# Output projection of a hybrid encoder layer: from 384-column blocks of single token tiles to 512-column blocks of pairs, three pairs by Strassen's seven products

## The chip, the cores and the metric

One core of one Trainium2 chip. The metric is device time in microseconds of one execution. The kernel before took 657.14 us, the median of three runs (655.28 to 658.43).

## What is computed

One encoder layer is applied to two sequences, a sample of 1024 tokens and a prompt of 512 tokens, each 1024 wide, in float32:

```python
h = rms_norm(x, norm_g)
proj = h @ w_in
u_pool, g_pool, q, k, v, g_attn = jnp.split(proj, ...)
pool_out = pool_mixer(u_pool, w_pool, pool_scale) * jax.nn.silu(g_pool)
attn_out = neighbourhood_attention(q, k, v, rpb) * jax.nn.silu(g_attn)
mixed = jnp.concatenate([pool_out, attn_out], axis=-1)
return x + mixed @ w_out
```

The change concerns the last line: `mixed` (1536 tokens in all, 1024 wide) times `w_out` (1024 x 1024), plus the residual `x`.

## The kernel before

**Precision.** Every float32 operand of a large matmul is split into a high part in the matmul's fast format (fp32r) and a low part that holds the rest (`split`, L426: the high part by ScalarE or VectorE, the low part by VectorE or GpSimd). A product is three matmuls into the same PSUM accumulator (`mm3`, L454): high by high, high by low, low by high.

**Stages.** The sample is done first and then the prompt, each in four passes over pairs of heads (L781 and L817). A pass loads a block of `w_in` and projects q, k and v (`project_qkv`), then the gates (`gate`, L631) and the pool input (`u_block`, L707), and does the attention of two heads (`attention`, L641) and one group of the pooling mixer (`pooling`, L715). Results go to a DRAM tensor `mixed` per sequence, channels on partitions. The output projection comes last (L828 to L861).

**The output projection.** `w_out` is cut into column blocks of 384, 384 and 256. For each block its eight chunks of 128 rows are loaded and split (`load_w`, L443). Then all 12 tiles of 128 tokens (8 of the sample, 4 of the prompt) go by: one accumulator each, eight chunks, three matmuls a chunk. The tokens' rows of `mixed` are loaded and split once, in the first block, into 24 half tiles `mt`, and all of them stay. The result leaves by a VectorE add of `x` from PSUM (tile `xr`) and a DMA of the block.

**What sets the order.** Nothing is issued while the program text runs. `Plan` records each operation, and `Plan.order` (L228) simulates the five engines with estimated durations (`Plan.cost`, L118) and issues in the order that the simulation gives, so every instruction has line L329 in the profile. When an engine is free it takes, of the operations whose inputs are ready, the one with the lowest priority number, then the one that comes first in the text. FIRST is -1 (weight splits, adds that free a PSUM accumulator), 0 is the default (attention and pooling among it), MAIN is 1: the large projections, which are also kept in the order of the text among themselves. So the large matmuls fill whatever TensorE time attention leaves. Within `plan.choice()` an operation goes to that engine on which it would end sooner. On the chip every engine runs its list in order.

**Buffers.** Tiles come from rings (`ring`, `big`, `halves`, `staged`): a new tile of a ring waits until all uses of the tile that many places before are done. The rings that matter here: `ht` with 16 slots of 2 x 512, holding the transposed inputs and later `mt`; `big` with 6 slots of 4 KB a partition; `w` with 10 and `wr` with 5 slots for weights and their raw loads; `raw` with 2 slots; `tree` with 2, used by the pooling; `qkv` with 4. PSUM has eight banks: three for `acc`, two each for `s` and `pt` and one for `po`, the last three used by attention.

Of the kernel before, what the change touches and what calls it, by code (L numbers as in the profile page):

```python
# [332 lines left out]
FIRST = -1  # L333
MAIN = 1
# [3 lines left out]
def encoder(ctx, tc, xn_p, xt_p, xn_s, xt_s, w_in, w_out, w_pool, pscale, ng, qg, kg,  # L338
            rpb, rpbm, negs, ident_d, ones_d, edge_d, y_p, y_s):
    plan = Plan(tc.nc)  # L340
# [18 lines left out]
    def staged(name):  # L359
        return ring("raw", 2, [P, 512], name)  # L360
# [65 lines left out]
    def split(out_h, out_l, src, scale=None):  # L426
        with plan.choice():
            act.activation(out=out_h, in_=src, func=AF.Copy, scale=1.0 if scale is None else scale)
            if scale is None:
                dve.tensor_copy(out=out_h, in_=src)  # L430
        low(out_l, src, out_h, scale)

    def low(out, src, high, scale=None):
        if scale is not None:
            dve.scalar_tensor_tensor(out=out, in0=src, scalar=scale, in1=high.bitcast(F32),
                                     op0=ALU.mult, op1=ALU.subtract)
            return
        with plan.choice():
            dve.tensor_tensor(out=out, in0=src, in1=high.bitcast(F32), op=ALU.subtract)
            if src.space != PSUM:  # L440
                pool.tensor_tensor(out=out, in0=src, in1=high.bitcast(F32), op=ALU.subtract)

    def load_w(blk, width, nm, chunks=range(KC), queue=sp):  # L443
        ws = []
        for k in chunks:
            raw = ring("wr", RAWS, [P, BW], f"wr_{nm}_{k}")[:, 0:width]
# [7 lines left out]
    def mm3(out, ah, al, bh, bl, first, last):  # L454
        pe.matmul(out, lhsT=ah, rhs=bh, start=first, stop=False)
        pe.matmul(out, lhsT=ah, rhs=bl, start=False, stop=False)
        pe.matmul(out, lhsT=al, rhs=bh, start=False, stop=last)
# [26 lines left out]
    ns_edge = {cb: sb.tile([P, 384], F32, name=f"ns_edge_{cb}") for cb in (0, 3)}  # L484
# [4 lines left out]
    class Sequence:  # L489
# [160 lines left out]
        def head_rows(self, p, hd, rt, bt):  # L650
# [4 lines left out]
            for cb in range(4):  # L655
# [13 lines left out]
                pe.matmul(sv, lhsT=q[:, hd, qo:qo + P], rhs=kv(k[:, hd]), start=True, stop=False)  # L669
                pe.matmul(sv, lhsT=q[:, hd, qo:qo + P], rhs=kv(k[:, 2 + hd]), start=False, stop=True)  # L670
# [158 lines left out]
    mts = {}  # L829
    f0 = 0  # L830
    for bi, fw in enumerate((384, 384, 256)):
        w = load_w(w_out[:, :, f0:f0 + fw], fw, f"o{bi}")
        for i, (sq, t, xn, y) in enumerate(toks):
            if bi == 0:
                mts[i] = []
                for hf in range(2):
                    nm = f"mt_{i}_{hf}"
                    if i < 8:
                        m = halves(nm)
                    elif i < 11:  # L840
                        m = big([P, 2, 512], nm, F32R)
                    else:
                        m = ring("v", 4, [P, 2, 512], nm, F32R)
                    if i < 5:
                        raw = staged(f"mr_{i}_{hf}")
                    else:
                        raw = bias[i % 2][:, hf * 512:hf * 512 + 512]
                    sp.dma_start(out=raw.rearrange("p (k s) -> p k s", s=P),
                                 in_=sq.mixed.rearrange("k p s -> p k s")[:, 4 * hf:4 * hf + 4, t * P:(t + 1) * P])
                    split(m[:, 0], m[:, 1], raw)  # L850
                    mts[i].append(m)
            acc = bank("acc", f"acco_{bi}_{i}")
            with plan.priority(MAIN):
                for c in range(KC):
                    m, mc = mts[i][c // 4], slice((c % 4) * P, (c % 4 + 1) * P)
                    mm3(acc[:, 0:fw], m[:, 0, mc], m[:, 1, mc], w[c][:, 0], w[c][:, 1], c == 0, c == KC - 1)
            xr = ring("qkv", QBUFS, [P, BW], f"xr_{bi}_{i}")[:, 0:fw]
            sp.dma_start(out=xr, in_=xn[t * P:(t + 1) * P, f0:f0 + fw])
            dve.tensor_tensor(out=xr, in0=acc[:, 0:fw], in1=xr, op=ALU.add)
            sp.dma_start(out=y[t * P:(t + 1) * P, f0:f0 + fw], in_=xr)  # L860
        f0 += fw  # L861
# [64 lines left out]
```

## Time and profile before

| | |
|---|---|
| median of three runs | 657.14 us (655.28 to 658.43) |
| the profiled execution | 655.92 us |
| its span, first to last instruction | 654.1 us |
| TensorE busy (PE) | 644.7 us, 99% |
| VectorE busy (DVE) | 514.6 us, 79% |
| ScalarE busy (ACT) | 346.4 us, 53% |
| GpSimd busy (POOL) | 64.3 us, 10% |
| moved by DMA | 97.35 MB, 149 GB/s |
| first matmul of the output projection | 510.0 us |

PE is TensorE's matmuls, PEld its weight loads, SP the engine that issues the DMAs. Names such as `acco<-w_o,mt` are the tiles that an instruction writes and reads: `acc_s` and `acc_p` are the q, k, v projections of sample and prompt, `accg` the gates, `accu` the pool inputs, `acco` the output projection, `s`, `pt` and `po` attention. Matmuls overlap in TensorE, so the mean duration of one is longer than the time that it takes from the next.

### The profile page before, as it was taken

What the parts mean: (1) busy time and instruction counts of PE and PEld (TensorE: products, weight loads), DVE (VectorE), ACT (ScalarE), POOL (GpSimd) and SP (SyncE); (2) the same over time, 40 slices, a digit from 0 to 9 for tenths busy, and PEclk for the clock granted to TensorE, in tenths of its full rate; (3) what the DMA queues carried; (4) which work ended last, traced back from release to release, by engine and by line L of the source; (5) the groups of instructions that cost most, each with busy time, mean ns of one, the idle gap of its engine ahead of it and who ended that gap; (6) DMA issues with size and microseconds to landing.
All of it is one profiled execution on the core that took longest, in us unless ns stands there. A gap on an engine that the chain in (4) does not pass through costs nothing.

```text
span 654.1 us, 11733 instructions
## 1 busy us (share of the span) xinstructions
PE 644.7 (99%) x3728; PEld 600.6 (92%) x3728; DVE 514.6 (79%) x1569; ACT 346.4 (53%) x837; POOL 64.3 (10%) x105
## 2 busy tenths in 40 slices
PE   6999999999999999999999999999999999999997
PEld 6998899989899888999889889899898999999997
DVE  6689899899987899969999889899999985411211
ACT  5755777567664666445686457674766740100100
POOL 1130101000000000100012310111211100000000
PEclk9999999999999999999999999999999999999999
DMA  8974254342374422425344544546556666533222
GB/s 291 351 216 138 93 182 120 117 122 83 95 234 139 149 75 61 139 94 171 93 118 145 154 149 149 160 151 193 167 176 208 195 206 217 157 98 98 85 93 73
DMA packets 90657, 97.35 MB, mean 149 GB/s; under 512 B 12644, under 2 KB 82404, under 8 KB 90596
## 3 DMA queue, kind: packets, MB, share of 16 engines
q1 hardware_dynamic: 90596, 96.61, 47.9%
q8 instruction: 29, 0.48, 0.3%
q14 instruction: 32, 0.26, 0.1%
HBM read 77.21 MB, written 19.37 MB: 148 GB/s over the span
## 4 chain that ended last, share of the span: by engine, by line
PE 98%; DMA 1%; DVE 0%; ACT 0%; issue 0%; SPq 0%; ACTq 0%
PE acc_s L329 21%; PE acco L329 21%; PE accg_s L329 14%; PE acc_p L329 10%; PE accu_s L329 7%; PE accg_p L329 7%; PE po_s L329 4%; PE accu_p L329 3%; PE pt_s L329 3%; PE s_s L329 3%; PE po_p L329 1%; PE s_p L329 1%; PE pt_p L329 1%; PE ptq_s L329 1%; PE accm_s L329 1%; PE ptq_p L329 1%
## 5 line engine op out<-in xcount | busy, mean ns | idle before, releaser
L329 PE MATMUL acc_s<-w_sA,ht_s 128*128 128x384 f32 x768 | 146.1, 343 | 5.9 <-DVE w_sA L329 5.9
L329 PEld LDWEIGHTS acc_s<-w_sA,ht_s 128*128 128x128 f32 x768 | 135.9, 191 | 7.2 <-ACT ht_s L329 5.5
L329 PE MATMUL acco<-w_o,mt 128*128 128x384 f32 (+1 forms) x864 | 136.8, 318 | 0.0
L329 PEld LDWEIGHTS acco<-w_o,mt 128*128 128x128 f32 x864 | 133.9, 188 | 0.5 <-DVE w_o L329 0.3
L329 PE MATMUL accg_s<-ht_s,w_sT 128*128 128x512 f32 x384 | 100.7, 399 | 0.0
L329 PEld LDWEIGHTS accg_s<-ht_s,w_sT 128*128 128x128 f32 x384 | 70.0, 188 | 11.9
L329 DVE TENSOR_TENSOR xr<-acco,xr 128x384 f32<-128x384 f32 (+1 forms) x36 | 18.3, 511 | 78.9 <-PE acco L329 78.9
L329 PE MATMUL acc_p<-w_pA,ht_p 128*128 128x384 f32 x384 | 77.6, 341 | 0.0
L329 PEld LDWEIGHTS acc_p<-w_pA,ht_p 128*128 128x128 f32 x384 | 65.9, 188 | 0.8
L329 PE MATMUL accu_s<-ht_s,w_sT 128*128 128x512 f32 x192 | 52.0, 398 | 0.0
L329 PE MATMUL accg_p<-ht_p,w_pT 128*128 128x512 f32 x192 | 46.2, 392 | 0.0
L329 ACT ACTIVATE w_o<-wr_o 128x384 fp32r<-128x384 f32 (+1 forms) x20 | 9.5, 485 | 67.7 <-PE acco L329 61.9
L329 PEld LDWEIGHTS accg_p<-ht_p,w_pT 128*128 128x128 f32 x192 | 35.7, 188 | 7.3
L329 ACT ACTIVATE k<-ptq_s,gqk 64x256 fp32r<-64x256 f32 x64 | 30.0, 470 | 22.1 <-PE ptq_s L329 21.3
L329 PEld LDWEIGHTS accu_s<-ht_s,w_sT 128*128 128x128 f32 x192 | 34.8, 188 | 5.4
L329 ACT ACTIVATE ns_s<-ns_s,sm_s 128x384 f32<-128x384 f32 x52 | 31.2, 610 | 7.5 <-DVE sm_s L329 7.1
L329 DVE TENSOR_TENSOR pp_s<-pt_s,pp_s 128x384 fp32r<-128x384 f32 x64 | 34.5, 545 | 0.5 <-ACT pp_s L329 0.4
L329 ACT ACTIVATE ns_edge<-ns_edge,sm_s 128x288 f32<-128x288 f32 x50 | 26.3, 530 | 15.8 <-DVE sm_s L329 15.4
L329 PE MATMUL po_s<-pp_s,v 128*128 128x256 f32 x192 | 32.2, 287 | 0.1
L329 PEld LDWEIGHTS po_s<-pp_s,v 128*128 128x128 f32 x192 | 28.9, 188 | 2.2 <-ACT w_pT L329 0.4
L329 PE MATMUL s_s<-k,q 128*128 128x288 f32 (+1 forms) x128 | 30.5, 327 | 0.0
L329 ACT ACTIVATE qkv_s<-acc_s,rr_s 128x384 f32<-128x384 f32 x24 | 13.8, 580 | 26.3 <-PE acc_s L329 22.6
(194 smaller groups left out, 1111.3 us busy)
## 6 DMA issues: line engine op xcount, KB each, us to landing
v<-vd_s SPq DMA_DIRECT2D x64, 128.0 KB
wr_sA<-in_w_in SPq DMA_DIRECT2D x32, 192.0 KB
wr_sT<-in_w_in SPq DMA_DIRECT2D x32, 192.0 KB
wr_pA<-in_w_in SPq DMA_DIRECT2D x32, 192.0 KB
wr_pT<-in_w_in SPq DMA_DIRECT2D x32, 192.0 KB
out<-xr SPq DMA_DIRECT2D x24, 192.0 KB
x<-in_xt_s SPq DMA_DIRECT2D x16, 256.0 KB
vd_s<-vt_s SPq DMA_DIRECT2D x32, 128.0 KB
```

The lines of the kernel that those rows point to most:

```text
L329: op.fn()
```

## The change

The 12 token tiles are taken in six pairs, and the columns in two halves of 512. `w_out` is then 2 x 2 blocks of 512 x 512 (B11, B12, B21, B22), and a pair's rows of `mixed` are 2 x 2 blocks of 128 x 512 (token by channel half).

The first three pairs (`PLAIN = 3`) are done plainly: for a pair and a column half two accumulators, four products of four chunks. The last three pairs use the Winograd form of Strassen's algorithm: seven products in place of eight, each again three matmuls a chunk. With S1 = A21 + A22, S2 = S1 - A11, S3 = A11 - A21, S4 = A12 - S2 and T1 = B12 - B11, T2 = B22 - T1, T3 = B22 - B12, and T4 = B21 - T2:

- C11 = A11 B11 + A12 B21
- C12 = A11 B11 + S2 T2 + S1 T1 + S4 B22
- C21 = A11 B11 + S2 T2 + S3 T3 + A22 T4
- C22 = A11 B11 + S2 T2 + S3 T3 + S1 T1

Sums of products are formed where they can be by accumulating on in a PSUM bank whose intermediate value has been read out: A11 B11 is copied to SBUF by ScalarE (`p1`) and added to the three residual tiles by GpSimd; VectorE adds bank b2 to a residual tile after S2 T2 and again after S3 T3. The first Strassen pair (`late`) does S4 B22 early and has it copied and subtracted (`p3`). The T's are made once from a second load of `w_out`, the S's for each pair, and all of them are split into high and low parts like the rest.

With this go changes of buffers: q and k become six tiles of a ring `kq`, which the T's take over; in the order of the `big` ring `sg` and `ph` change places, so that `sg` takes the slot of the second `more` tile (copies of the first pass's q, k, v) in place of `ph`; residual tiles and copies (`piece`) come from the rings `tree`, `pp` and `raw`; B and part of T lie in `ht`, which no longer holds all rows. Two estimates of `Plan.cost` change: GpSimd's power function, which this kernel doesn't use, and GpSimd's other operations, now 200 ns plus the elements' time in place of 135.

```diff
-                return 1600
-            return 135 + n * (2.35 if out.dtype == F32R else 1.85)
+                return 715 + n * 119
+            return 200 + n * (2.35 if out.dtype == F32R else 1.85)
...
-    sg = big([P, 1024], "sg")
+    ph = big([P, 2, 512], "ph", F32R)
     U = big([P, 2 * 528], "U")
     sgp = big([P, 1024], "sgp")
-    ph = big([P, 2, 512], "ph", F32R)
+    sg = big([P, 1024], "sg")
...
-    q = sb.tile([P, 2, 1024], F32R, name="q")
-    k = sb.tile([P, 4, 1024], F32R, name="k")
+    q = [ring("kq", 6, [P, 1024], f"q_{i}", F32R) for i in range(2)]
+    k = [ring("kq", 6, [P, 1024], f"k_{i}", F32R) for i in range(4)]
...
+    def raw_part(nm, i, j, c, half):
+        nm = f"{nm}_{c}_{half}"
+        raw = (ring("qkv", QBUFS, [P, BW], nm) if half and nm[1] == "T" else raw_w(nm))[:, 0:256]
+        o = 512 * j + 256 * half
+        sp.dma_start(out=raw, in_=w_out[:, 4 * i + c, o:o + 256])
+        return raw
+    def weights(nm, i, j, new):
+        with plan.priority(FIRST):
+            ws = [new(f"{nm}_{c}") for c in range(4)]
+            for c, w in enumerate(ws):
+                for half in range(2):
+                    cols = slice(256 * half, 256 * half + 256)
+                    split(w[:, 0, cols], w[:, 1, cols], raw_part(f"r{nm}", i, j, c, half))
+        return ws
...
+    def tt(out, a, b, op):
+        with plan.choice():
+            for eng in (dve, pool):
+                eng.tensor_tensor(out=out, in0=a, in1=b, op=op)
...
+    def product(acc, a, w, first, last, **kw):
+        with plan.priority(MAIN):
+            for c in range(4):
+                mm3(acc, a.chunk(0, c), a.chunk(1, c), w[c][:, 0], w[c][:, 1], first and c == 0, last and c == 3, **kw)
...
+    def leave(tok, j, acc, x):
+        _, t, _, y = toks[tok]
+        with plan.priority(FIRST):
+            dve.tensor_tensor(out=x, in0=acc, in1=x, op=ALU.add)
+        sp.dma_start(out=y[t * P:(t + 1) * P, j * 512:(j + 1) * 512], in_=x)
...
+    B = {(0, 1): weights("B12", 0, 1, halves)}
+    plain, left = {}, [halves(f"left_{i}") for i in range(4)]
...
+    def plain_block(tok, j):
+        accs = [bank("acc", f"acco_{tok + r}_{j}") for r in range(2)]
+        for hf in range(2):
+            for r in range(2):
+                product(accs[r], plain[tok + r][hf], B[hf, j], hf == 0, hf == 1)
+        for r in range(2):
+            leave(tok + r, j, accs[r], x_piece(tok + r, j))
+    for tok in range(4):
+        plain_rows(tok, left if tok < 2 else None)
+        if tok == 1:
+            B[1, 1] = weights("B22", 1, 1, halves)
+            B[0, 0] = weights("B11", 0, 0, halves)
+            B[1, 0] = weights("B21", 1, 0, lambda nm: big([P, 2, 512], nm, F32R))
+    for tok, j in ((0, 1), (2, 1), (0, 0), (2, 0)):
+        plain_block(tok, j)
+    if PLAIN == 3:
+        for tok in (4, 5):
+            plain_rows(tok, left)
+        for j in range(2):
+            plain_block(4, j)
+    T1, T2, T3, T4 = T = [[], [], [], []]
+    for c in range(4):
+        t1, t2, t3, t4 = [(ring("kq", 6, [P, 2, 512], f"T_{c}_{i}", F32R) if 4 * c + i < 6 else
+                           ring("v", 4, [P, 2, 512], f"T_{c}_{i}", F32R) if 4 * c + i < 10 else
+                           big([P, 2, 512], f"T_{c}_{i}", F32R) if 4 * c + i < 12 else
+                           halves(f"T_{c}_{i}")) for i in range(4)]
+        for half in range(2):
...
+            tt(b22, b22, b12, ALU.subtract)
+            tt(b12, b12, b11, ALU.subtract)
+            tt(b11, b22, b11, ALU.add)
+            tt(b21, b21, b11, ALU.subtract)
...
+    for tok in range(2 * PLAIN, 12, 2):
+        odd, late = tok // 2 % 2, tok == 2 * PLAIN
...
+        a11, s1, s2, a12, s3 = [Rows(f"{n}_{tok}") for n in ("A11", "S1", "S2", "A12", "S3")]
+        a22, s4 = [Rows("", t) for t in left[2 * odd:2 * odd + 2]]
...
+        b1, b2, b3 = [bank(("s", "s", "pt")[i] if odd else "acc", f"acco_{tok}_{i}") for i in range(3)]
...
+        product(b1, a11, B[0, 0], True, False, **part)
+        with plan.priority(FIRST):
+            act.activation(out=p1, in_=b1, func=AF.Copy)
+        pool.tensor_tensor(out=x21, in0=x21, in1=p1, op=ALU.add)
+        if late:
+            product(b3, s4, B[1, 1], True, False, **part)
...
+        product(b2, s2, T2, True, False, **part)
+        with plan.priority(FIRST):
+            dve.tensor_tensor(out=x12, in0=b2, in1=x12, op=ALU.add)
+        pool.tensor_tensor(out=x12, in0=x12, in1=p1, op=ALU.add)
+        product(b1, a12, B[1, 0], False, True, **part)
+        leave(tok, 0, b1, x11)
+        product(b2, s3, T3, False, False, **part)
+        with plan.priority(FIRST):
+            dve.tensor_tensor(out=x22, in0=b2, in1=x22, op=ALU.add)
+        pool.tensor_tensor(out=x22, in0=x22, in1=p1, op=ALU.add)
...
+        product(b3, s1, T1, not late, late, **part)
+        leave(tok + 1, 1, b3, x22)
...
+        product(b2, a22, T4, False, True, **part)
+        leave(tok + 1, 0, b2, x21)
+        if not late:
+            product(b3, s4, B[1, 1], False, True, **part)
+            leave(tok, 1, b3, x12)
```

More of the change, by code (lines that the diff above doesn't have):

```diff
@@ L40 @@
 QBUFS = 4
+PLAIN = 3
 class Plan:
@@ L441, in low, with raw_w @@
                 pool.tensor_tensor(out=out, in0=src, in1=high.bitcast(F32), op=ALU.subtract)
+    def raw_w(name):
+        return ring("wr", RAWS, [P, BW], name)
     def load_w(blk, width, nm, chunks=range(KC), queue=sp):
@@ L445, in load_w @@
         for k in chunks:
-            raw = ring("wr", RAWS, [P, BW], f"wr_{nm}_{k}")[:, 0:width]
+            raw = raw_w(f"wr_{nm}_{k}")[:, 0:width]
             queue.dma_start(out=raw, in_=blk[:, k])
@@ L452, in load_w, with mm3 @@
         return ws
[L454 to L457, printed above, removed]
+    def mm3(out, ah, al, bh, bl, first, last, **kw):
+        pe.matmul(out, lhsT=ah, rhs=bh, start=first, stop=False, **kw)
+        pe.matmul(out, lhsT=ah, rhs=bl, start=False, stop=False, **kw)
+        pe.matmul(out, lhsT=al, rhs=bh, start=False, stop=last, **kw)
     def rsqrt(y, t, ms):
@@ L614, in project_qkv @@
                     for rows in (own[hd], own[1 - hd]):
-                        v = q[rows, hd, qa].rearrange("p (cb r c) -> p r cb c", cb=4, r=8)
+                        v = q[hd][rows, qa].rearrange("p (cb r c) -> p r cb c", cb=4, r=8)
                         q_dst.append(v[:, lo::-1, :, ::-1] if hi < 0 else v[:, lo:hi:-1, :, ::-1])
@@ L618, in project_qkv @@
                     for rows in (own[hd], own[1 - hd]):
-                        act.activation(out=k[rows, hd, ka], in_=k_src[hd], func=AF.Copy, scale=gqk[own[hd]])
+                        act.activation(out=k[hd][rows, ka], in_=k_src[hd], func=AF.Copy, scale=gqk[own[hd]])
                     act.activation(out=q_dst[2 * hd], in_=q_src[hd], func=AF.Copy)
                 for hd in range(2):
-                    low(k[own[hd], 2 + hd, ka], k_src[hd], k[own[hd], hd, ka], gqk[own[hd]])
+                    low(k[2 + hd][own[hd], ka], k_src[hd], k[hd][own[hd], ka], gqk[own[hd]])
                     low(q_dst[2 * hd + 1], q_src[hd], q_dst[2 * hd])
@@ L668, in head_rows @@
                 sv = s[:, 0:self.kt_rows * n]
-                pe.matmul(sv, lhsT=q[:, hd, qo:qo + P], rhs=kv(k[:, hd]), start=True, stop=False)
-                pe.matmul(sv, lhsT=q[:, hd, qo:qo + P], rhs=kv(k[:, 2 + hd]), start=False, stop=True)
+                pe.matmul(sv, lhsT=q[hd][:, qo:qo + P], rhs=kv(k[hd]), start=True, stop=False)
+                pe.matmul(sv, lhsT=q[hd][:, qo:qo + P], rhs=kv(k[2 + hd]), start=False, stop=True)
                 ns = (ns_edge[cb] if cb in ns_edge else ring("ns", 2, [P, 384], f"ns_{nm}"))[:, 0:KEYS]
@@ L774, in encoder @@
     for hd in range(2):
-        pool.memset(k[HD - hd * HD:P - hd * HD, 2 + hd].bitcast(F32), 0.0)
+        pool.memset(k[2 + hd][HD - hd * HD:P - hd * HD].bitcast(F32), 0.0)
     for t in ns_edge.values():
@@ L825, in encoder @@
         pr.pooling(p)
-    toks = [(ss, t, xn_s, y_s) for t in range(8)] + [(pr, t, xn_p, y_p) for t in range(4)]
[L829 to L861, printed above, removed]
@@ new lines, in encoder, with __init__, parts, span @@
+    class Rows:
+        def __init__(self, nm, tile=None):
+            self.tiles = [tile] if tile else [ring("w", WBUFS, [P, 2, 256], f"{nm}_{i}", F32R) for i in range(2)]
+            self.n = 4 // len(self.tiles)
+        def parts(self, raw):
+            for i, x in enumerate(self.tiles):
+                n = P * self.n
+                split(x[:, 0, 0:n], x[:, 1, 0:n], raw[:, i * n:i * n + n])
+            return self
+        def span(self, part, c, n=2):
+            return self.tiles[c // self.n][:, part, c % self.n * P:(c % self.n + n) * P]
+        def chunk(self, part, c):
+            return self.span(part, c, 1)
@@ new lines, in tt, with row_raw @@
+    def tt(out, a, b, op):
+        with plan.choice():
+            for eng in (dve, pool):
+                eng.tensor_tensor(out=out, in0=a, in1=b, op=op)
+    def row_raw(raw, tok, half):
+        sq, t = toks[tok][:2]
+        sp.dma_start(out=raw.rearrange("p (k s) -> p k s", s=P),
+                     in_=sq.mixed.rearrange("k p s -> p k s")[:, 4 * half:4 * half + 4, t * P:(t + 1) * P])
+        return raw
+    def product(acc, a, w, first, last, **kw):
+        with plan.priority(MAIN):
+            for c in range(4):
+                mm3(acc, a.chunk(0, c), a.chunk(1, c), w[c][:, 0], w[c][:, 1], first and c == 0, last and c == 3, **kw)
@@ new lines, in encoder, with piece, x_piece @@
+    spare = [0]
+    def piece(nm):
+        i = spare[0]
+        spare[0] += 1
+        tag = "t" if i < 4 * PLAIN else "prt"[i // 2 % 3]
+        return (ring("pp", 2, [P, 512], nm) if tag == "p" else
+                ring("tree", 2, [P, 528], nm)[:, 0:512] if tag == "t" else staged(nm))
+    def x_piece(tok, j):
+        _, t, xn, _ = toks[tok]
+        x = piece(f"xr_{tok}_{j}")
+        sp.dma_start(out=x, in_=xn[t * P:(t + 1) * P, j * 512:(j + 1) * 512])
+        return x
+    def leave(tok, j, acc, x):
[3 more added lines that the diff above has]
+        sp.dma_start(out=y[t * P:(t + 1) * P, j * 512:(j + 1) * 512], in_=x)
@@ new lines, in encoder, with plain_rows @@
+    toks = [(ss, t, xn_s, y_s) for t in range(8)] + [(pr, t, xn_p, y_p) for t in range(4)]
+    B = {(0, 1): weights("B12", 0, 1, halves)}
+    plain, left = {}, [halves(f"left_{i}") for i in range(4)]
+    def plain_rows(tok, tiles=None):
+        plain[tok] = [Rows(f"a_{tok}_{hf}", tiles and tiles[2 * (tok % 2) + hf]).parts(
+            row_raw(staged(f"ra_{tok}_{hf}"), tok, hf)) for hf in range(2)]
+    def plain_block(tok, j):
[5 more added lines that the diff above has]
+            leave(tok + r, j, accs[r], x_piece(tok + r, j))
@@ new lines, in encoder @@
+    T1, T2, T3, T4 = T = [[], [], [], []]
[5 more added lines that the diff above has]
+        for half in range(2):
+            cols = slice(256 * half, 256 * half + 256)
+            b11, b12, b22, b21 = [raw_part(f"rT{i}{j}", i, j, c, half) for i, j in ((0, 0), (0, 1), (1, 1), (1, 0))]
+            tt(b22, b22, b12, ALU.subtract)
+            tt(b12, b12, b11, ALU.subtract)
+            tt(b11, b22, b11, ALU.add)
+            tt(b21, b21, b11, ALU.subtract)
+            for x, raw in zip((t1, t2, t3, t4), (b12, b11, b22, b21)):
+                split(x[:, 0, cols], x[:, 1, cols], raw)
+        for x, t in zip((t1, t2, t3, t4), T):
+            t.append(x)
@@ new lines, in encoder @@
+    for tok in range(2 * PLAIN, 12, 2):
+        odd, late = tok // 2 % 2, tok == 2 * PLAIN
+        (r11, r12), (r21, r22) = [[row_raw(bias[r][:, hf * 512:hf * 512 + 512], tok + r, hf) for hf in range(2)]
+                                  for r in range(2)]
+        a11, s1, s2, a12, s3 = [Rows(f"{n}_{tok}") for n in ("A11", "S1", "S2", "A12", "S3")]
+        a22, s4 = [Rows("", t) for t in left[2 * odd:2 * odd + 2]]
+        a11.parts(r11)
+        a22.parts(r22)
+        a12.parts(r12)
+        tt(r22, r21, r22, ALU.add)
+        tt(r21, r11, r21, ALU.subtract)
+        tt(r11, r22, r11, ALU.subtract)
+        tt(r12, r12, r11, ALU.subtract)
+        if late:
+            s4.parts(r12)
+        s2.parts(r11)
+        s3.parts(r21)
+        s1.parts(r22)
+        if not late:
+            s4.parts(r12)
+        part = dict(skip_group_check=True)
+        b1, b2, b3 = [bank(("s", "s", "pt")[i] if odd else "acc", f"acco_{tok}_{i}") for i in range(3)]
+        p1 = piece(f"p1_{tok}")
+        x11, x12, x21, x22 = [x_piece(tok + r, j) for r in range(2) for j in range(2)]
+        product(b1, a11, B[0, 0], True, False, **part)
+        with plan.priority(FIRST):
+            act.activation(out=p1, in_=b1, func=AF.Copy)
+        pool.tensor_tensor(out=x21, in0=x21, in1=p1, op=ALU.add)
+        if late:
+            product(b3, s4, B[1, 1], True, False, **part)
+            p3 = piece(f"p3_{tok}")
+            with plan.priority(FIRST):
+                act.activation(out=p3, in_=b3, func=AF.Copy)
+        product(b2, s2, T2, True, False, **part)
[5 more added lines that the diff above has]
+        product(b2, s3, T3, False, False, **part)
+        with plan.priority(FIRST):
+            dve.tensor_tensor(out=x22, in0=b2, in1=x22, op=ALU.add)
+        pool.tensor_tensor(out=x22, in0=x22, in1=p1, op=ALU.add)
+        if late:
+            pool.tensor_tensor(out=x22, in0=x22, in1=p3, op=ALU.subtract)
+        product(b3, s1, T1, not late, late, **part)
+        leave(tok + 1, 1, b3, x22)
+        if late:
+            leave(tok, 1, b3, x12)
+        product(b2, a22, T4, False, True, **part)
+        leave(tok + 1, 0, b2, x21)
+        if not late:
+            product(b3, s4, B[1, 1], False, True, **part)
+            leave(tok, 1, b3, x12)
```

## The prediction

> **What bounds the kernel now.** I read the page's shares first, then busy time by stretch, then the chain of waits in order of time, then the costliest groups with shapes kept apart.
>
> ```profile
> PE 644.7 (99%) x3728; PEld 600.6 (92%) x3728; DVE 514.6 (79%) x1569; ACT 346.4 (53%) x837; POOL 64.3 (10%) x105
> ```
>
> TensorE is busy 644.7 of the span of 654.1 us. A share can hide stages, so the same by stretches (columns: length, then busy time of PE, PEld, DVE, ACT, POOL, granted clock, DMA share, GB/s):
>
> ```profile
> 60.00:100.00 40.00, 40.00 (x232) 36.22 (x231) 37.31 (x120) 28.60 (x72) 3.28 (x5) 1.00 0.43 135
> 100.00:200.00 100.00, 100.00 (x583) 92.73 (x582) 90.11 (x293) 66.27 (x164) 5.82 (x11) 1.00 0.43 130
> 200.00:343.00 143.00, 143.00 (x805) 130.06 (x804) 129.01 (x402) 83.96 (x202) 10.32 (x16) 1.00 0.38 114
> 343.00:450.00 107.00, 106.86 (x609) 98.37 (x608) 99.19 (x302) 67.64 (x173) 20.17 (x29) 1.00 0.50 153
> 450.00:509.80 59.80, 59.80 (x322) 53.02 (x321) 57.28 (x179) 39.16 (x98) 12.84 (x16) 1.00 0.63 189
> 509.80:530.00 20.20, 20.20 (x126) 18.91 (x125) 19.40 (x64) 14.43 (x40) 0.37 (x2) 1.00 0.59 182
> 530.00:560.00 30.00, 30.00 (x175) 30.00 (x174) 17.01 (x32) 3.87 (x7) 0.00 (x0) 1.00 0.65 205
> 560.00:600.00 40.00, 40.00 (x231) 40.00 (x230) 9.63 (x20) 2.35 (x5) 0.00 (x0) 1.00 0.38 122
> 600.00:650.80 50.80, 50.80 (x386) 50.62 (x385) 10.17 (x23) 2.09 (x5) 0.00 (x0) 1.00 0.27 90
> 650.80:654.10 3.30, 0.02 (x1) 0.00 (x0) 0.42 (x1) 0.00 (x0) 0.00 (x0) 0.95 0.12 40
> ```
>
> From 60 us on PE has work in every stretch at full clock. The last 3.3 us are the final add and its output transfer. The output projection is the stretch from 509.8: for 20 us it shares PE with the last attention heads, then it has PE alone, with DVE, ACT and DMA mostly idle. So time is what PE is given to do, and any PE time removed there comes off the end, as long as the helpers keep up. Between 60 and 509.8 DVE is busy 37.31 + 90.11 + 129.01 + 99.19 + 57.28 = 412.9 of 449.8 us: that is the second bound, with 36.9 us of room.
>
> Now the price of one matmul by its width. The chain of waits, in order of time (start, length, piece), gives stretches in which one kind of matmul runs undisturbed; the 256-wide one comes from the timeline:
>
> ```profile
> 207.24 8.67 PE acc_s L329 x50
> 492.28 5.50 PE accg_p L329 x24
> 529.65 121.17 PE acco L329 x790
> 650.85 0.42 DVE xr L329
> ```
>
> ```profile
> 635.74 15.08 PE L329 MATMUL acco<-w_o,mt 128*128 128x256 f32 x128
> ```
>
> 384 columns: 8.67/50 = 173.4 ns. 512 columns: 5.50/24 = 229.2 ns. 256 columns: 15.08/128 = 117.8 ns. Per column that is 0.452, 0.448 and 0.460 ns: wide ones are slightly cheaper. The means in the groups below (337, 280 ns) are latencies that overlap, not prices.
>
> **Part 1: PE's own work.** Groups with shapes kept apart:
>
> ```profile
> L329 PE MATMUL acco<-w_o,mt 128*128 128x384 f32 x576 | 103.1, 337 | 0.0
> L329 PE MATMUL acco<-w_o,mt 128*128 128x256 f32 x288 | 33.9, 280 | 0.0
> L329 DVE TENSOR_TENSOR mt<-bias,mt 128x512 fp32r<-128x512 f32 x14 | 9.6, 689 | 2.5 <-ACT mt L329 2.2
> L329 DVE TENSOR_TENSOR w_o<-wr_o,w_o 128x256 fp32r<-128x256 f32 x8 | 3.3, 422 | 0.6 <-ACT w_o L329 0.2
> L329 ACT ACTIVATE mt<-bias 128x512 fp32r<-128x512 f32 x9 | 5.6, 628 | 14.2 <-DMA bias<-mixed_p 5.9 <-DMA bias<-mixed_s 4.4 <-DVE xr L329 3.8
> L329 ACT ACTIVATE w_o<-wr_o 128x256 fp32r<-128x256 f32 x7 | 2.9, 418 | 48.1 <-PE acco L329 45.9 <-DMA wr_o<-in_w_out 1.9
> ```
>
> Before: 864 matmuls, of which 790 take 121.17 us and the other 74, all 384 wide, lie between attention's: 74 x 173.4 ns = 12.8. Together 134.0 us. After: a plain pair is 2 tokens x 2 column halves x 8 chunks x 3 = 96 matmuls of 512 columns; a Strassen pair is 7 products x 4 chunks x 3 = 84. Three of each: 540. At 229.2 ns that is 123.8 us, **10.2 us less**. Width alone gives 576 x 229.2 = 132.0, so 2.0 us; the three missing products (36 matmuls) give 8.2 us.
>
> The Trainium skill (TensorE: Matmul & The Clock Gate, Back-to-back issue gap) puts a warm matmul at N/2.4 + 2.5 ns, so 162.5, 109.2 and 215.8 ns; by it the stage would go from 125.0 to 116.5, an estimate of 8.5 us gained. The rows above are 6 to 8% dearer at each width, and the measurement decides.
>
> **Part 2: the tail.** The last add becomes 512 wide, and the last transfer 256 KB in place of 128 KB.
>
> ```profile
> L329 DVE TENSOR_TENSOR ze<-accg_p,Rb_s 128x512 f32<-128x512 f32 x8 | 5.5, 687 | 1.4 <-PE accg_p L329 1.4
> GB/s 143 25 0 0 0 0 143 324 62 16 12 0 0 0 0 0 0 78 344 103 0 0 0 0 0 0 0 0 123 336 66 0 0 0 0 0 0 0 0 0
> ```
>
> A 512-wide add from PSUM takes 0.69 us against 0.42 in the chain: +0.27. The second line is DMA traffic from 645 to 655 us in slices of 0.25 us: the last 128 KB pass in the three slices from 652.0, at up to 336 GB/s, so another 131 KB is +0.39. Together **+0.7**. C12's add is alone at the end: the other three blocks leave before it.
>
> **Part 3: helpers' added work.** All on DVE, ACT, POOL and DMA, beside PE. DVE from 510 on, taking every low part and every sum there: B 32 lows x 0.42 = 13.4; T 32 sums and 32 lows x 0.42 = 26.9; plain rows 12 x 0.69 = 8.3; a Strassen pair 4 sums x 0.69 + 10 lows x 0.42 + 2 lows x 0.69 = 8.3, three times 25.0; 24 exits and 6 early drains x 0.69 = 20.7. Sum 94 us, in 124 us of projection; before, DVE had 36.8 us of work in the 120.8 us from 530 (17.01 + 9.63 + 10.17). High parts go mostly to ACT: 64 x 0.42 + 12 x 0.63 + 30 x 0.42 + 6 x 0.63 = 51 us. Neither is full. SP issues 136 transfers in place of 120, and w_out is read twice, 4 MB more, in a stage that moved 90 to 205 GB/s (above), where the kernel's first two slices of 40 reach 291 and 351:
>
> ```profile
> GB/s 291 351 216 138 93 182 120 117 122 83 95 234 139 149 75 61 139 94 171 93 118 145 154 149 149 160 151 193 167 176 208 195 206 217 157 98 98 85 93 73
> ```
>
> Cost 0. If a helper did bind, the cost is one of the rivals.
>
> **Part 4: where a product waits.** (a) In a Strassen pair bank b2 is written by three products, with one product on another bank between each. Each gap is 12 x 229.2 = 2.75 us, and the DVE add that reads b2 must fit; the ScalarE copy of b1 has the same gap. (b) At the hand-over from plain to Strassen, S4 overwrites the rows that the very last plain product reads, and is the second product: it has product A11, 2.75 us, in which to do one exit add 0.69, a high 0.63 and a low 0.69 = 2.0. (c) T's fourth chunk takes B12's place, which is read last 5.5 us before the plain blocks end; T2's fourth chunk is wanted 5.5 + 2 x 2.75 + 2.1 = 13 us later, for eight splits of 256, 8 x 0.84 = 6.7 us. All fit, so I take 0 for each, and +0.4 us for semaphores and small misfits; the nearest row is what the projection's weight loads stood idle before:
>
> ```profile
> L329 PEld LDWEIGHTS acco<-w_o,mt 128*128 128x128 f32 x864 | 133.9, 188 | 0.5 <-DVE w_o L329 0.3
> ```
>
> That is 0.5 us. The bounds are 0 (no wait of PE is there to be removed, so there is nothing to gain) and the late drains' 2.3 below.
>
> (d) The first block's second x tile shares a slot of the tree ring with the last pooling:
>
> ```profile
> 524.69 0.66 DVE L329 TENSOR_TENSOR ph<-tree_p,ph 128x512 fp32r<-128x512 f32 x1
> ```
>
> ```profile
> 1.17 3.29 DMA x<-in_xt_s
> ```
>
> The slot comes free at 525.4; with the 3.3 us of the chain's only load of that size (256 KB, at the start), the add is possible at 528.7. In the 19.8 us up to 529.65 acco had 12.8 us, 65% of PE. The block wants 11.0 us, so it ends at 509.8 + 11.0/0.65 = 526.7, and the third bank carries another 2.75 us of products, to 531. Covered, by about 2 us.
>
> (e) sg moves in the ring of large tiles to the place of the second `more` tile:
>
> ```profile
> L329 DVE SCALAR_TENSOR_TENSOR sg<-ze x12: 669/684/696, 51.6 to 499.3; 128x512 f32<-128x512 f32 x12
> L329 DVE TENSOR_TENSOR vt_s<-more,vt_s x3: 278/285/396, 59.6 to 70.1; 128x128 fp32r<-128x128 f32 x3
> L329 DVE TENSOR_TENSOR sg<-pv_s,sg x32: 397/418/1168, 83.5 to 369.8; 64x256 f32<-64x256 f32 x32
> ```
>
> sg's first write, at 51.6, must now wait until `more` is read out, 70.4. Behind it ze is held, and the second gate's accumulator with it: one bank of three for 19 us. The two u blocks drain through U, not ze, and run on the other two; attention reads sg at 83.5 only. Cost 0; with the cover gone, PE would lose about 3 us at 68 to 71. q and k as six ring tiles: same reads and writes, 0.
>
> **Sum**: -10.2 + 0.7 + 0.4 = -9.1. The profiled execution took 655.92, 1.2 below the median of 657.14, within the spread of 655.28 to 658.43; on its own time this gives 646.8, on the median **648.0 us**.
>
> **Rivals.** *Late drains.* The Strassen pairs put POOL adds (x + p1) beside DVE work for the first time in this stage.
>
> ```profile
> 505.00 1.06 POOL L329 TENSOR_TENSOR tree_p<-U 128x527 f32<-128x527 f32 x1 [10.55 <-DVE U L329]
> 51.08 0.16 DVE L329 SCALAR_TENSOR_TENSOR st_s<-st_s 128x8 f32<-128x8 f32 x1
> 51.64 1.09 POOL L329 TENSOR_TENSOR s_s<-more 128x256 f32<-128x256 f32 x1 [4.57 <-DVE st_s L329]
> 52.16 0.59 DVE L329 SCALAR_TENSOR_TENSOR st_s<-st_s 128x8 f32<-128x8 f32 x1
> 518.33 0.68 DVE L329 TENSOR_TENSOR tree_p<-tree_p 128x513 f32<-128x513 f32 x1
> ```
>
> A DVE operation of 0.16 us, issued while POOL was at work, took 0.59 and ended when POOL did. So a queued sum can stand for a POOL add of 1.06 before it runs: 1.06 + 0.69 + the drain 0.69 = 2.44, inside 2.75. With two queued, 3.13: 0.38 late, at most six times, 2.3 us: 650.3. Against: the planner puts drains FIRST. The Trainium skill (SBUF — State Buffer, Who interferes with whom) says so too: DVE with two SBUF inputs and a GpSimd instruction that reads SBUF lock each other out for a whole instruction. The trace agrees, by the 0.59 us.
>
> *Late start.* The splits of B11 and B21 go ahead of pooling: 16 x 0.42 = 6.7 us on a DVE that has 19.40 of 20.20 us filled. Then (d)'s add comes at 535.4, its cover ends at 531, and PE loses 4 us: 652, or 655 if the second block's rows come a product (2.75) late as well.
>
> *DVE becomes the bound before 510* (ends slower). POOL's operations are now costed 65 ns dearer, so the planner gives some to DVE, which has 36.9 us of room and is 92% full. A 513-wide add is 0.68 on DVE, 1.06 on POOL: all of POOL's 64.3 us would be 41 us of DVE. If all went and a third of the room could not be used, PE waits 41 - 25 = 16 us: 664. It outweighs the gain once the waits pass 9 us, that is once DVE's share there nears 98%. Against: 65 ns on choices worth 600 and more flips few of them.
>
> *It doesn't do what it says*: the counts above follow from the loops; no room for it.
>
> **Chances.** Forecast 0.72. Late drains 0.08, late start 0.10, DVE the bound 0.10. A change of under 0.5% (3.3 us) is what this measurement can't tell from none, so faster means below 653.85: the forecast 0.72, drains 0.07, start 0.07 = 0.86. Same: 0.01 + 0.03 + 0.03 = 0.07. Slower: 0.07, the rest of DVE's case. The range takes the gain whole with the run spread below it (657.14 - 10.2 - 1.9 = 645.0) and reaches past the late start's first step (653.0).
>
> **What would show it.** Right: 540 accumulating matmuls of 512 columns in the projection at 229 ns, PE gap-free to the end, span near 645; POOL and DVE busy shares up only after 510. Drains late: PE gaps of 0.3 to 0.5 us ended by DVE before S3 or A22. Late start: PE waiting for a DVE add on an accumulator at about 531. DVE bound: PE gaps before 510 and the first acco matmul later than 510. The forecast is wrong if acco's matmuls cost over 235 ns each, or PE idles more than 2 us after 60 us.

## The result

The changed kernel takes 648.15 us (median of four runs, 647.79 to 648.98) where the kernel before, in the same series, takes 657.49 (655.28 to 658.43): ratio 0.9865, 95% interval 0.9837 to 0.9892. A second series gives 649.01 against 656.64, ratio 0.9882 (0.9861 to 0.9902). So 7.6 to 9.3 us are gained; the forecast was 648.0 in the range of 645.0 to 653.0.

The profiled execution took 648.40 us, with a span of 646.6 us: 7.5 less than the profiled one of before. The page of the changed kernel:

```profile
span 646.6 us, 11390 instructions
PE 635.0 (98%) x3404; PEld 567.0 (88%) x3404; DVE 557.1 (86%) x1647; ACT 372.8 (58%) x910; POOL 100.6 (16%) x142
```

3728 - 3404 = 324 matmuls are gone: 864 became 540, as counted. DVE has 42.5 us more to do and POOL 36.3. By stretches (columns as in the prediction):

```profile
509.80:540.00 30.20, 29.92 (x146) 24.26 (x145) 26.38 (x73) 18.43 (x51) 11.06 (x16) 1.00 0.80 249
540.00:560.00 20.00, 20.00 (x99) 16.51 (x98) 17.75 (x47) 12.46 (x34) 9.46 (x11) 1.00 0.78 238
560.00:581.40 21.40, 21.40 (x95) 17.57 (x94) 16.90 (x45) 5.74 (x14) 1.60 (x3) 1.00 0.59 190
581.40:589.00 7.60, 7.04 (x31) 5.26 (x30) 7.60 (x10) 3.41 (x8) 5.74 (x5) 1.00 0.41 139
589.00:642.90 53.90, 53.87 (x236) 43.83 (x234) 31.36 (x52) 9.11 (x20) 16.41 (x14) 1.00 0.39 127
```

The reader is to see that PE stays full, and that DVE, which before was busy for 17.01 of the 30 us from 530 and 9.63 of the 40 from 560, is now 85% busy up to 581 and has no gap at all from 581.4 to 589, the hand-over to Strassen. Pieces of the chain of waits in the projection:

```profile
549.82 31.62 PE acco L330 x138
588.08 54.81 PE acco L330 x238
642.91 0.69 DVE xr L330
```

A 512-wide matmul costs 31.62/138 = 229.1 ns in the plain part and 54.81/238 = 230.3 in the Strassen part. The busy time of one long stretch, first before and then after, gives the gaps:

```profile
60.00:640.00 580.00, 579.86 (x3362) 539.31 (x3361) 467.72 (x1425) 308.38 (x761) 52.80 (x79) 1.00 0.46 139
```

```profile
60.00:640.00 580.00, 578.44 (x3117) 514.79 (x3116) 511.13 (x1499) 334.43 (x834) 89.86 (x116) 1.00 0.48 147
```

PE idles 1.56 us there in place of 0.14. The account of the two profiled executions: 10.2 us of matmuls less, 1.4 of new gaps, 0.4 of gaps before 60 us (busy 53.04 of 53.42 from 6.58 to 60, full before), and a tail of 646.6 - 642.9 = 3.7 in place of 3.3. That makes -8.0 where -7.5 was measured: PE's busy time fell by 9.7 (644.7 to 635.0) and not by 10.2, and where that half microsecond went is not shown.

### The profile page after: what moved, and what is told of

It is laid out like the page before. It is cut to its first block, busy times and chain, and to the rows that moved or that the text cites. A ratio compares the mean times of both kernels' runs of the same rounds, so it can differ in the third digit from the quotient of the medians.

```text
span 646.6 us, 11390 instructions
## 1 busy us (share of the span) xinstructions
PE 635.0 (98%) x3404; PEld 567.0 (88%) x3404; DVE 557.1 (86%) x1647; ACT 372.8 (58%) x910; POOL 100.6 (16%) x142
## 4 chain that ended last, share of the span: by engine, by line
PE 91%; DVE 4%; DMA 3%; issue 1%; ACT 0%; SPq 0%; DVEq 0%; ACTq 0%
PE acc_s L330 21%; PE acco L330 15%; PE accg_s L330 14%; PE acc_p L330 10%; PE accu_s L330 7%; PE accg_p L330 6%; PE po_s L330 4%; PE accu_p L330 3%; PE pt_s L330 3%; PE s_s L330 3%; DMA xr<-in_xn_s 1%; PE po_p L330 1%; PE ptq_s L330 1%; DVE B L330 1%; PE pt_p L330 1%
## 5 line engine op out<-in xcount | busy, mean ns | idle before, releaser
L330 PE MATMUL acc_p<-w_pA,ht_p 128*128 128x384 f32 x384 | 75.4, 339 | 0.7 <-DVE w_pA L330 0.5
L330 PE MATMUL acco<-B,left 128*128 128x512 f32 x228 | 56.2, 395 | 0.6 <-DVE left L330 0.6
L330 PEld LDWEIGHTS acco<-B,left 128*128 128x128 f32 x228 | 41.9, 188 | 9.5 <-DVE left L330 1.0
L330 PE MATMUL accg_p<-ht_p,w_pT 128*128 128x512 f32 x192 | 47.6, 395 | 0.0
L330 DVE TENSOR_TENSOR xr<-acco,xr 128x512 f32<-128x512 f32 x30 | 20.5, 686 | 20.4 <-PE acco L330 18.2
L330 ACT ACTIVATE ns_edge<-ns_edge,sm_s 128x288 f32<-128x288 f32 x54 | 28.4, 529 | 16.5 <-DVE sm_s L330 16.3
L330 POOL TENSOR_TENSOR vt_s<-qkv_s,vt_s 128x128 fp32r<-128x128 f32 x17 | 9.1, 540 | 122.0 <-ACT vt_s L330 97.3
```

The source lines that it names most:

```text
L330: op.fn()
```

## The experiments

Ratios are to the kernel before, run in the same series on the same chip; each series has its own median of before, 656.0 to 657.2.

**The changed kernel once more**, unedited.

> The changed kernel itself, as the reference for its neighbours on the same chip: 648 us. Where the time went is compared with it in this call.

649.01 us (647.97 to 649.29). Its profiled execution has more gaps than the first one of the same kernel: 2.36 us of PE from 60 to 640, in place of 1.56.

```profile
60.00:640.00 580.00, 577.64 (x3112) 513.75 (x3110) 512.03 (x1498) 334.21 (x834) 90.09 (x116) 1.00 0.48 147
```

**All pairs plain.**

```diff
-PLAIN = 3
+PLAIN = 6
...
+    for t0 in range(4, 2 * PLAIN, 2):
+        for tok in (t0, t0 + 1):
+            plain_rows(tok, left if t0 // 2 % 2 == 0 else None)
+        for j in range(2):
+            plain_block(t0, j)
...
-    for c in range(4):
+    for c in range(4 if PLAIN < 6 else 0):
```

> All six pairs in plain 512-wide blocks, no T and no S (576 matmuls in place of 540; rows of the later pairs alternate between the two sets of tiles). Theory (TensorE's own time decides): 36 x 229.2 ns = 8.2 us more than the changed kernel, about 656.4, with two thirds of DVE's added work gone. Rival (the gain came from the width, the buffers or the new order): within 2 us of the changed kernel, about 649. Rival (Strassen's helpers already cost TensorE time in the changed kernel): clearly less than 8 us slower, say 3 to 5, about 652.

656.35 us (654.60 to 658.55), ratio 0.9989 (0.9973 to 1.0004): 7.3 us slower than the changed kernel of the same series, where 8.2 were expected. From its page and over the long stretch:

```profile
PE 642.4 (98%) x3440; PEld 573.9 (88%) x3440; DVE 520.3 (80%) x1581; ACT 350.2 (54%) x854; POOL 62.9 (10%) x104
60.00:640.00 580.00, 578.37 (x3120) 515.63 (x3119) 474.42 (x1433) 312.11 (x778) 51.71 (x78) 1.00 0.46 139
```

PE idles 1.63 us in the stretch, as much as in the changed kernel (1.56), so the difference does not lie in gaps that another order brought: it is PE's busy time, 642.4 against 635.0. The gain is Strassen's; the 512-wide blocks with all the new buffers, by themselves, can't be told from the kernel before. There the width was to give 2.0 and the tail to cost 0.7; the interval, -1.8 to +0.3 us, holds the difference but does not show it.

**A product left out.** The edit removes one line; C21 and C22 of the three pairs then lack S3 T3.

```diff
-        product(b2, s3, T3, False, False, **part)
```

> The product S3 T3 is left out of each Strassen pair (C21 and C22 lack it), all helpers stay. Theory: 36 matmuls less at 229.2 ns, 8.2 us less than the changed kernel, about 639.9. Rival (the Strassen pairs go by their helpers, DVE and POOL, not by TensorE): less than half of that, 644 or more.

641.33 us (639.71 to 641.95): 7.7 us less, nearly the whole price of 36 matmuls, with every helper still there. The Strassen part goes by TensorE.

**Four Strassen pairs.**

```diff
-PLAIN = 3
+PLAIN = 2
```

> PLAIN = 2: four Strassen pairs, 528 matmuls. Theory: 12 x 229.2 = 2.75 us less than the changed kernel, about 645.4, as long as the T's are ready 22 us earlier. Rival (helpers bind: DVE is 85 to 90% full from 510 to 560): the T's come late, TensorE waits for them, and the time is 650 or more.

661.62 us, ratio 1.008 (1.0064 to 1.0096): one more Strassen pair saves 2.75 us of matmuls and loses 12.6 in all. Waits of PE, the timeline of PE at the place, and the stretches around it:

```profile
PE acco L330 <- ACT left L330: 13.4, 1, 13.4
```

```profile
578.80 5.49 PE L330 MATMUL acco<-B,left 128*128 128x512 f32 x12 [13.44 <-ACT left L330]
584.09 3.31 PE L330 MATMUL acco<-T,S 128*128 128x512 f32 x12
587.24 2.92 PE L330 MATMUL acco<-B,A 128*128 128x512 f32 x12
```

```profile
562.40:578.80 16.40, 2.96 (x13) 2.07 (x12) 15.42 (x30) 7.76 (x20) 8.87 (x10) 0.67 0.38 118
578.80:584.10 5.30, 5.30 (x13) 4.02 (x14) 1.82 (x4) 0.42 (x1) 1.37 (x2) 0.50 0.67 195
584.00:585.00 1.00, 1.00 (x4) 0.72 (x3) 0.34 (x1) 0.60 (x1) 0.00 (x0) 0.54 0.02 7
585.00:586.00 1.00, 1.00 (x6) 0.82 (x5) 0.78 (x2) 0.00 (x0) 0.00 (x0) 1.00 0.00 0
```

PE stands for 13.4 us until S4 (tile `left`) is split, while DVE is busy 15.42 of 16.40 us, mostly with the T's. Then the wait is paid a second time: for 5.3 us the granted clock is 0.50, and S4's twelve matmuls take 5.49 us from the first start to the last end, and the next twelve 3.31, where twelve take 2.92 after that. 13.4 + 2.6 + 0.4 = 16.4, and 645.4 + 16.4 = 661.8. The Trainium skill (TensorE: Matmul & The Clock Gate, What's actually happening) has the clock fall to one half after an idle window of about 3.4 us, and return after a busy one. The run agrees with the halving; the return took some 6 us, as the mean of 0.54 from 584 to 585 and the 1.00 behind it show.

**The same with S4's work put first.**

```diff
+        with plan.priority(FIRST if late else 0):
             (r11, r12), (r21, r22) = ...
...
+        with plan.priority(FIRST if late else 0):
             a11.parts(r11)
...
             if late:
                 s4.parts(r12)
```

(all sums and splits between these lines are in the block.)

> PLAIN = 2 with the first Strassen pair's loads, sums and splits put ahead of the T's (priority FIRST). In the run with four pairs TensorE waited 13.4 us for S4, whose sums stood behind the T's on DVE, and went on at half clock. Theory (DVE's whole work up to there is the bound): S4 comes in time, the wait moves to T2, whose last chunk is done at about 577 where TensorE wants it at 570: 5 to 8 us, 650 to 654. Rival (only the place of S4 in the order was wrong): 12 x 229.2 ns less than the changed kernel, 645 to 646.

657.37 us, ratio 1.0003 (0.9992 to 1.0014). The wait moved as the theory had it, but its size was put too small. Waits of PE, and the stretch around them:

```profile
PE acco L330 <- ACT T L330: 7.1, 2, 5.7
PE acco L330 <- DVE T L330: 1.3, 2, 0.9
```

```profile
562.50:582.00 19.50, 11.11 (x40) 7.89 (x39) 17.32 (x39) 8.35 (x21) 6.84 (x7) 0.78 0.57 174
```

The wait has moved to the T's, 8.4 us, again with a lowered clock (mean 0.78). Against the 645.4 looked for, four pairs lost 16.2 us. S4's place in the order was 4.2 of them. Of the other 12.0 the trace shows 8.4 as waits for the T's, from a DVE that is busy 17.32 of 19.50 us, and 1.9 as slow matmuls (40 take 11.11 us where 9.2 is usual); the rest is not accounted for.

**T's splits done twice**, three Strassen pairs.

```diff
             for x, raw in zip((t1, t2, t3, t4), (b12, b11, b22, b21)):
-                split(x[:, 0, cols], x[:, 1, cols], raw)
+                for _ in range(2):
+                    split(x[:, 0, cols], x[:, 1, cols], raw)
```

> PLAIN = 3, and every split of a T is done twice (64 further operations of 256 columns; 32 of them low parts, 13.4 us on DVE or twice that on POOL). Theory now (the T's come just in time, DVE having 10.6 us of room between 509.8 and 581.4): TensorE waits at the hand-over, 3 to 8 us, 651 to 656. Rival (the prediction's view: DVE needs 94 of 124 us, so there are 30 us of room): no change, 648 to 649.

662.27 us, ratio 1.0076 (1.0058 to 1.0095): 13 to 14 us slower than the changed kernel. Waits of PE:

```profile
PE acco L330 <- ACT left L330: 6.1, 1, 6.1
PE acco L330 <- DVE A L330: 4.7, 1, 4.7
```

10.8 us of waiting, for A11 and for S4, whose splits stand behind the T's on DVE. S4's twelve matmuls again take 5.49 us. The prediction's view of the helpers falls: at the hand-over there is no room, although over the whole stage there is.

**The residual adds on DVE.**

```diff
-        pool.tensor_tensor(out=x21, in0=x21, in1=p1, op=ALU.add)
+        dve.tensor_tensor(out=x21, in0=x21, in1=p1, op=ALU.add)
```

(and so for the other adds of p1 and p3.)

> The ten adds of p1 and p3 to the residual tiles go to DVE in place of POOL: 10 x 0.69 = 6.9 us more on DVE after 585, and POOL no longer stands in DVE's way there. Theory (TensorE decides, all of this is covered): within 1 us of the changed kernel, 648 to 649. Rival (drains made late by POOL's adds cost time): 1 to 2 us faster. Rival (DVE is the bound in the Strassen part too): 2 us or more slower.

649.25 us (647.93 to 649.78), the same as the changed kernel. After the hand-over neither DVE's amount of work nor POOL's standing in its way sets the time, in this order.

**Rows first and the last output in halves**, three Strassen pairs: the FIRST block shown above, and

```diff
-            leave(tok, 1, b3, x12)
+            for o in range(0, 512, 256):
+                with plan.priority(FIRST):
+                    dve.tensor_tensor(out=x12[:, o:o + 256], in0=b3[:, o:o + 256], in1=x12[:, o:o + 256], op=ALU.add)
+                sp.dma_start(out=y[t * P:(t + 1) * P, 512 + o:768 + o], in_=x12[:, o:o + 256])
```

(the second for the last pair only.)

> PLAIN = 3 with the first Strassen pair's loads, sums and splits put first, and the last output leaving as two halves of 256 columns. Theory: the 0.6 us wait for S4's low part goes and the last transfer is half as long, 0.3 us: 0.5 to 1 us less than the changed kernel, 647.5 to 648.5. Rival (T2 is then late in its turn): the same or 1 us slower.

650.42 us (648.31 to 651.07): a miss. The wait for S4's low part is still there, 0.55 us, and the last piece of PE ends at 644.9 of a span of 648.7: 3.8 us of tail, no less than the 3.7 with the last transfer whole. Priority could not move S4 here. What holds it shows in the timeline of the changed kernel:

```profile
578.69 0.62 ACT L330 ACTIVATE left<-bias 128x512 fp32r<-128x512 f32 x1
580.12 0.69 DVE L330 TENSOR_TENSOR left<-bias,left 128x512 fp32r<-128x512 f32 x1
580.84 0.69 DVE L330 TENSOR_TENSOR bias<-bias 128x512 f32<-128x512 f32 x1
...
582.07 0.68 DVE L330 TENSOR_TENSOR bias<-bias,bias 128x512 f32<-128x512 f32 x1
...
583.56 1.23 DVE L330 TENSOR_TENSOR bias<-bias,bias 128x512 f32<-128x512 f32 x1
...
585.32 0.67 DVE L330 TENSOR_TENSOR bias<-bias 128x512 f32<-128x512 f32 x1
585.32 2.16 POOL L330 TENSOR_TENSOR S<-bias,S 128x256 fp32r<-128x256 f32 x2 [1.08 <-ACT S L330]
...
586.80 1.23 DVE L330 TENSOR_TENSOR left<-bias,left 128x512 fp32r<-128x512 f32 x1
...
588.08 2.56 PE L330 MATMUL acco<-B,left 128*128 128x512 f32 x10 [0.56 <-DVE left L330]
```

The first two lines are the split of A22. Only then can the four sums run (the `bias` lines), because they are made in place of the raw rows, and S4 is the last of them; then its low part, then PE. And A22 itself waited for its place, which token 5's rows held: their last reader is two products of 2.75 us ahead of the end of the plain blocks at 584.0, so it ends at 578.5.

**Earlier places.**

```diff
-        a22, s4 = [Rows("", t) for t in left[2 * odd:2 * odd + 2]]
+        a22, s4 = [Rows("", t) for t in left[2 - 2 * odd:4 - 2 * odd]]
```

> A22 and S4 of the first Strassen pair take the places of token 4's rows in place of token 5's, which are read 2.75 us earlier in the last plain block (and the later pairs the other two). The sums are made in place, so S4's chain starts only when A22 has been split into its place: A22's place, not S4's own, is what made S4 late. Theory: the 0.56 us wait for S4's low part is gone from the trace, the time 0.5 us less than the changed kernel. Rival (DVE's queue, full of T's splits, sets the moment): the wait stays.

648.23 us (647.64 to 649.14), ratio 0.9875 (0.9856 to 0.9894). The timeline there, A22's high part and PE:

```profile
576.09 0.43 DVE L330 CAST left<-bias 128x512 fp32r<-128x512 f32 x1 [0.43 <-PE acco L330]
...
584.27 2.91 PE L330 MATMUL acco<-B,A 128*128 128x512 f32 x12
587.02 2.88 PE L330 MATMUL acco<-B,left 128*128 128x512 f32 x12
589.74 2.45 PE L330 MATMUL acco<-T,S 128*128 128x512 f32 x10
```

A22's split starts 2.6 us earlier, as soon as PE has left its place, and S4's product follows A11's without a gap. So A22's place was what held the chain, as far as one edit can show it: the planner also gave one of the four sums to POOL here. The half microsecond in the total is below what these runs resolve.

**The old estimate for POOL**, in the changed kernel.

```diff
-            return 200 + n * (2.35 if out.dtype == F32R else 1.85)
+            return 135 + n * (2.35 if out.dtype == F32R else 1.85)
```

> The changed kernel with the old estimate for POOL (135 ns in place of 200). Theory: the order changes, TensorE's work doesn't: within 1 us of the changed kernel, 648 to 649; the small waits at w_pA (0.7 us) and at the start may go. Rival (the estimate is where part of the gain comes from): 2 us or more slower.

653.96 us (652.70 to 655.84), ratio 0.9964 (0.9947 to 0.9980): 5 to 6 us of the gain are gone with the same 540 matmuls. From 60 to 640 us:

```profile
60.00:640.00 580.00, 574.13 (x3092) 509.73 (x3091) 512.61 (x1495) 326.05 (x817) 104.36 (x134) 1.00 0.48 147
```

PE idles 5.87 us in place of 1.56, in several places. The second longest of them is a late drain; lines of the timeline:

```profile
611.95 0.43 DVE L330 CAST left<-bias 128x512 fp32r<-128x512 f32 x1 [0.63 <-DMA bias<-mixed_p]
...
613.86 0.74 POOL L330 TENSOR_TENSOR A<-bias,A 128x256 fp32r<-128x256 f32 x1 [5.63 <-ACT A L330]
613.92 1.95 DVE L330 TENSOR_TENSOR bias<-bias,bias 128x512 f32<-128x512 f32 x2
...
616.72 0.69 DVE L330 TENSOR_TENSOR xr<-acco,xr 128x512 f32<-128x512 f32 x1
617.46 0.74 PE L330 MATMUL acco<-T,S 128*128 128x512 f32 x2 [1.40 <-DVE xr L330]
```

PE waits 1.4 us for the drain, which stands behind the next pair's splits and sums in DVE's list. DVE had waited 0.63 us for the load of their rows, and two of the sums, 0.69 each, took 1.95 us beside a low part on POOL, 0.6 too long. So a sum held up by POOL is one half of it, as in the rival, and a late load the other.

**The new estimate alone**, in the kernel before: the same line, the other way.

> The kernel before with the new estimate for POOL alone. Theory: within 1 us of the kernel before, 656 to 658, with the w_pA waits of the changed kernel if the estimate makes them. Rival (DVE as the second bound before 510): slower by 2 us or more; or, if the estimate was part of the gain, 2 us or more faster.

659.16 us (657.93 to 660.35), ratio 1.0040 (1.0026 to 1.0055): 2.5 us slower. PE idles 3.19 us from 60 to 640:

```profile
60.00:640.00 580.00, 576.81 (x3338) 536.02 (x3337) 472.14 (x1429) 307.05 (x758) 43.45 (x71) 1.00 0.46 139
```

So the estimate is no gain of its own; it suits the changed kernel and hurts the other.

**A dearer estimate still.**

```diff
-            return 200 + n * (2.35 if out.dtype == F32R else 1.85)
+            return 265 + n * (2.35 if out.dtype == F32R else 1.85)
```

> The changed kernel with POOL's estimate raised once more, by the same 65 ns, to 265. On the chip POOL's 256-wide low parts of S took 1.06 us where 200 gives 0.80 and 265 gives 0.87. Theory (dearer is nearer to the truth, so the planner's order has fewer misfits): 647 to 649, as with 200. Rival (any other order shifts a few small waits in or out by chance, whichever way the estimate moves): away from 648.5 by more than 1.5 us, with waits for DVE that the changed kernel doesn't show.

653.21 us (650.79 to 654.97), ratio 0.9948 (0.9930 to 0.9965). The rival holds: 135 and 265 both cost about 5 us against 200, in waits that stand elsewhere each time. PE idles 6.36 us from 60 to 640; three of its waits:

```profile
PE po_p L330 <- issue: 1.8, 1, 1.8
PE ptq_p L330 <- DVE qkv_p L330: 1.2, 1, 1.2
PE acco L330 <- DVE xr L330: 0.8, 1, 0.8
```

None of these three is in the changed kernel, and what ended the longest the profile does not show. The value of 200 is not nearer to the chip in any way that these runs show; it gives an order with fewer misfits.

## Why the prediction was right, and where it was only lucky

**Part 1, PE's work**, held: 540 matmuls at 229.1 to 230.3 ns. Undoing Strassen cost 7.3 us of the 8.2, and taking another 36 matmuls out gave 7.7. Of the 2.0 us for the width nothing can be seen in the total: all plain and before differ by less than their spread.

**Part 2, the tail**: +0.4, not +0.7. The wider add cost its 0.27. From the end of the add to the end of the span it is 2.8 us before and 3.0 now, so 0.2 in place of the 0.39 for a transfer twice as large, and 3.0 also with that transfer halved. That its size matters was not borne out.

**Part 3, helpers at cost 0**, is right for this kernel by a margin of nothing. It compared 94 us of DVE work with the 124 us of the whole stage, but S4 and the T's are due when the plain blocks end, at 584.0, or a product or two later. Nor can DVE do all of it ahead, though it is busy only 61.0 of the 71.6 us up to 581.4: the last chunk of the T's and A22 go into places that the last plain block still reads. DVE stands for 1.79 us until the first of these is free, and from there to S4's product it is full:

```profile
576.70 0.29 DVE L330 CAST T<-rT 128x256 fp32r<-128x256 f32 x1 [1.79 <-PE acco L330]
576.70:588.10 11.40, 10.84 (x48) 8.39 (x46) 11.33 (x22) 5.80 (x14) 4.84 (x5) 1.00 0.33 111
```

One Strassen pair more, or the T's splits twice, and PE waits 11 to 13 us, and then goes at half clock.

**Part 4(a)** held in this order only. With the residual adds moved to DVE nothing changed, but under the old estimate a late drain cost 1.4 us at one place, more than the rival's 0.38, as the work ahead of it in DVE's list had itself been held up, by POOL and by a load.

**Part 4(b)** is the step that failed, in mechanism if not in weight. It gave S4 an exit add, a high and a low part, 2.0 of 2.75 us, and left out that S4 is the fourth of four sums made in place, behind A22's split. The chain was 0.56 us late, and with A22's place free earlier it was not.

**Part 4(c)** and **(d)** held: no product waited for a T in the changed kernel, whose last chunk was split from 576.7 to 580.2, and from 509.8 to 540 PE idles 0.28 us in all, so the late start is not there.

**Part 4(e)** held: sg's first write comes at 70.9 us (70.4 was the earliest allowed), and PE has no gap from 60 to 100.

```profile
L330 DVE SCALAR_TENSOR_TENSOR sg<-ze x12: 674/684/1195, 70.9 to 500.5; 128x512 f32<-128x512 f32 x12
```

**The 0.4 us for misfits** was too little (1.4 of new gaps after 60 us, and 2.2 in the second profiled execution, whose 2.36 us of idle PE are past the 2 us that the prediction named as a sign of being wrong). Its bounds, 0 to 2.3, were far too narrow: other orders of the very same work cost 5 us more. Waits of half a microsecond to two, in several places, are a term of the sum that the prediction did not have. The forecast of 648.0 met the median because -10.2 + 0.4 + 1.4 + 0.4 = -8.0 lies within 1.1 of its -9.1, and the kernel before varies by more than that. There is luck in it: the estimate for POOL was changed together with the blocks. With the old one in both kernels the change gains 2.7 us (656.64 to 653.96), with the new one in both 10 to 11 (659.16 to between 648.15 and 649.01, across series). Nothing in the sum of the prediction tells an estimate of 200 from one of 135 or 265, and those gave 653.96 and 653.21, just outside its range.

**The rival that DVE binds before 510** is not there: from 60 to 509.8 DVE is busy 411.8 us in the changed kernel and 412.9 before, and PE's new gaps in that stretch are 0.6 us. The dearer estimate by itself slows the kernel before by 2.5 us, far from the 16.

## What to carry to other kernels

Work taken from the engine that is the bound comes off the end nearly one for one (7.3 and 7.7 us of 8.2 here), and its price can be read from the rows of a stretch in which that engine runs undisturbed. For the helpers that buy it, compare work with time between the moment at which their buffers come free and the moment at which the first result is due, not over the whole stage, and follow in-place buffers back to what frees the first of them. Where a planner sets the order by estimated costs, any edit reshuffles it: a 65 ns change of one estimate was worth 5 us here in either direction, so compare an edit under several orders before a few microseconds are put down to it.

## What was not expected of the hardware

A wait of PE costs twice: after 13.4 us of idling the next twelve matmuls took 5.49 us in place of 2.92, at a granted clock of 0.50. And POOL's work and DVE's hold each other up, as the prediction feared for the sums, and a plain copy is held too: lines of the changed kernel's timeline just after the hand-over:

```profile
585.32 2.16 POOL L330 TENSOR_TENSOR S<-bias,S 128x256 fp32r<-128x256 f32 x2 [1.08 <-ACT S L330]
586.80 1.23 DVE L330 TENSOR_TENSOR left<-bias,left 128x512 fp32r<-128x512 f32 x1
587.60 1.56 POOL L330 TENSOR_TENSOR xr<-xr,p 128x512 f32<-128x512 f32 x1
587.95 1.51 DVE L330 CAST left<-bias 128x512 fp32r<-128x512 f32 x1
```

A low part on DVE that took 0.69 us for A22 took 1.23 here: it was issued while POOL's two low parts ran, to 587.5. POOL's add, issued before that one ended, took 1.56 (1.06 for one of that length in the kernel before). A copy on DVE that took 0.42 to 0.43 in other places took 1.51 from its issue, beside that add. The Trainium skill (SBUF — State Buffer, Who interferes with whom) says that a VectorE copy in its fast mode and a GpSimd instruction exclude each other for a whole instruction; 1.51 us, ending 0.3 after POOL's add, agrees.
